# Dilated attention on one core: class keys only where the local scores lack them, counted in the local mask

## Chip, core and metric

The kernel runs on one core of a Trainium2 chip. The metric is the device time of one execution in microseconds (us), as the median of several runs. A profile is one further execution, recorded by the hardware profiler; its own time and its span are given beside the median.

## The reference

One decoder layer on x of 1024 positions by 1024 features, in float32. RMSNorm, one input projection, then two mixers side by side: a gated DeltaNet (4 heads of 128) and a dilated sliding-window attention (8 heads of 64). Their outputs go through one output projection; a gated MLP with a short causal convolution follows, and a last RMSNorm.

The change touches the attention alone. Every query t attends in three branches (window, dilation) = (128, 1), (512, 4), (2048, 16): to the keys t, t−d, t−2d, … back to t−window. The branches are merged by their softmax denominators:

```python
for window, dil in DIL_PATTERNS:
    ...
    num, den, m = band_attention(stride(qf), stride(kf), stride(vf), window // dil)
...
num_tot = wts[0][..., None] * nums[0] + wts[1][..., None] * nums[1] + wts[2][..., None] * nums[2]
den_tot = wts[0] * dens[0] + wts[1] * dens[1] + wts[2] * dens[2]
out = num_tot / den_tot[..., None]
```

With the weights written out this is one softmax over the union of the branches' keys in which a key that m branches want counts m times, that is, in which log m is added to its score. As 1024 positions are shorter than the window of 2048, the third branch reaches back to position 0.

## The kernel before, in words

**Stages.** The input projection comes first, and its products with the DeltaNet's chains; then attention runs beside the rest of the input projection (columns of later head pairs, then the four z columns of the DeltaNet's gate); then the output projection (`out_proj`, L1073), the MLP's up-projection (`mlp_up`, L1306) and down-projection (`mlp_down`, L1556). Big products are done in three passes with operands split in a high and a low part (`mm3`, L196; `split`, L202): names with hi and lo. Products of attention are plain float32 (`mm`, L188), which the profile shows as two records each; a transpose (`tp`, L192) is one record.

**Attention** (`attention`, L879) treats the 8 heads as four pairs (`pi`), and a pair's 1024 queries as 8 blocks of 128 (`n`), in two halves of four (`hh`). Inside a block the positions are ordered by class, that is by t mod 4 (4 classes of 32). Two blocks go through the stages together (`pair`): blocks 0 and 1, 2 and 3, 4 and 5, 6 and 7.

- *Local scores* (`scores`, L898): 128 queries against the keys of their own block and the one before (`n1` columns: 128 for block 0, 256 otherwise), for each of the two heads (`e`), which sit in the two halves of the array's rows.
- *Class scores* (L912): each class's 32 queries against the keys of the same class, in class blocks of 128 keys (class block 0: positions 0 to 511, class block 1: 512 to 1023). `nb` class blocks are taken, 1 in the first half and 2 in the second. There are 4 classes times 2 heads of these products, each on its own 64 by 32 piece of the array.
- *Softmax* (`softmax`, L922; `normalise`, L930): one VectorE operation per head adds the mask to the scores in PSUM and finds the row's extreme, one ACT operation takes the exponential and its sum, VectorE divides (tiles sm and mx). The row is `wd` = `n1` + 128 `nb` long. The local part's mask stands for branch 1, the class part's for branches 2 and 3; there a key wanted by both has 8 log 2 (the scale is 1/8).
- *Turn* (`turn`, L952): the probabilities are transposed in pieces of 128 columns (`wd` / 128 for each head); VectorE copies the local ones to pt, ACT the class ones to pb (`turned`, L944).
- *Values* (`values`, L966): pt times the local values, summed in one PSUM bank (`po`) per half. *Class values* (`merge_classes`, L975): when the half's four blocks are there, pb of all four blocks (128 columns: 4 times 32 queries of one class) against the class's values, for each class, class block and head; the two heads sit in the two halves of the array's columns. `give` (L987) copies the result out (oT).

`advance` (L1002) makes a pipeline: the turn of the pair of blocks before, the scores of this one, the values of the one before.

**What sets the order.** The order of TensorE's instructions is fixed when the program is built. A planner (`Weave`, L46) runs generators as streams with levels; each product adds its cost in us to a clock (`product`, L88), each operation of VectorE, ACT and SP to its engine's (`account`, L78). A stream that yields comes back when its operands should be ready, and the ready stream of the lowest level goes next. Attention has level 5, the input projection (`dense`, L486) level 9, so projection products (ps<-xhi, xlo with whi, wlo in the profile) fill the time in which attention would wait. `mm` stamps each product into that order (L189). The other engines' order is made by the framework's scheduler; attention's operations on VectorE and ACT have high priority there (`uv`, `ua`, L151).

**The end of attention.** `mixer_splits` (L1048) and `out_proj` start in the plan when the input projection is done: `mixer_splits` splits the mixers' outputs (tiles ohi and olo, in the slots of xhi and xlo), `out_proj` loads and splits the output projection's weights (wst<-in_wo, then whi on ACT and wlo on VectorE; two staging slots, two slots each for whi and wlo, and a third pair in slots of pb). The first two output columns are begun with the input parts that are there; the last one is the attention's.

Of the kernel before, what the change touches and what calls it, by code (L numbers as in the profile page):

```python
# [9 lines left out]
AF = mybir.ActivationFunctionType  # L10
# [11 lines left out]
NEG = -1.0e30  # L22
# [122 lines left out]
def hybrid_layer(tc, I, out):  # L145
# [6 lines left out]
    ua = Engine(wv, nc.scalar, "scalar", 0.12, 0.00085, first=tc.high_priority)  # L152
# [35 lines left out]
    def mm(dst, lhs, rhs, us, start=True, stop=True, **kw):  # L188
        tc.stamp_issue_order_token(nc.tensor.matmul(dst, lhs, rhs, start=start, stop=stop, **kw).ins, TOKEN)  # L189
        wv.product(us, dst, lhs, rhs)  # L190
# [54 lines left out]
    def bank(tag, name="ps"):  # L245
        return tile_(pp_, (P, 512), F32, name, tag, 2)
# [602 lines left out]
    def by_block(t):  # L849
        return t.rearrange("p (n c u) -> p n c u", n=NCH, c=4)  # L850
# [25 lines left out]

    HALVES = (slice(0, 64), slice(64, 128))

    def attention():  # L879
        for h in range(2):  # L880
            yield from wv.until(("c", h, NCH - 1))
# [8 lines left out]

        def mask(n):

            i, o, step, w, m = {0: (0, 128, 352, 128, 2), 1: (1, 0, 128, 128, 3), 2: (1, 384, 128, 128, 3),
                                3: (0, 608, 128, 128, 3)}.get(n, (0, 0, 480 - 32 * n, 256, 2))
            t = mks[i]
            return bass.AP(tensor=t.tensor, offset=t.offset + o, ap=[t.ap[0], [step, m], [1, w]]), m

        def scores(pair):  # L898

            for it, tag in zip(pair, ("asc", "atr")):  # L900
                it["k0"] = max(it["n"] - 1, 0) * P
                it["n1"] = (it["n"] + 1) * P - it["k0"]
                it["wd"] = it["n1"] + P * it["nb"]
                it["ps"] = [bank(tag) for _ in range(2)]
            yield wv.need(*pair[0]["ps"], *pair[1]["ps"], pair[0]["q"], pair[0]["k"])
            for it in pair:
                n, k0, n1_ = it["n"], it["k0"], it["n1"]
                for e, er in enumerate(HALVES):
                    mm(it["ps"][e][:, :n1_], it["q"][er, n * P:(n + 1) * P], it["k"][er, k0:k0 + n1_], 0.00085 * n1_)
            for it in pair:  # L910
                n, n1_, wd = it["n"], it["n1"], it["wd"]
                for c in range(4):  # L912
                    o = slice(32 * c, 32 * c + 32)
                    for e, er in enumerate(HALVES):
                        mm(it["ps"][e][o, n1_:wd].rearrange("p (n u) -> p n u", u=32),
                           it["q"][er, n * P + 32 * c:n * P + 32 * c + 32], by_block(it["k"])[er, :4 * it["nb"], c, :],
                           0.00022 * (wd - n1_), tile_position=(64 * e, 32 * c))
                ends = softmax(it)
            while put_off:
                gate(*put_off.pop(0), ends)  # L920
# [23 lines left out]
        def turned(it, e, pt, pp):  # L944
            wd, n1_ = it["wd"], it["n1"]
            inst = uv.tensor_copy(pt[:, :n1_], pp[:, :n1_])
            if it["g"]["pi"] == 3 and it["n"] > 5:
                for lo in last.get("wlo", ()):
                    after(lo, inst, "the probabilities go first")
            ua.activation(it["pb"][e][:, it["u"]].rearrange("p b t -> p (b t)"), pp[:, n1_:wd], AF.Copy)  # L950

        def turn(pair):  # L952
            pts = A("pt", "dv*", shape=(P, 4, 256))
# [21 lines left out]
        def merge_classes(g):  # L975
            vcv = g["vc"].rearrange("p (c b d) -> p c b d", c=4, b=2)
            po, nb = g["po"], g["nb"]
            yield wv.need(*g["pb"], slack=-PSLACK)
            for c in range(4):
                for b in range(nb):  # L980
                    for e in range(2):
                        er = slice(64 * e, 64 * e + 64)
                        mm(po[er].rearrange("p (u t) -> p u t", u=4)[:, :, 32 * c:32 * c + 32],
                           vcv[:, c, b, er], g["pb"][e][:, :, b, 32 * c:32 * c + 32], 0.14,
                           False, c == 3 and b == nb - 1, skip_group_check=True)

        def give(g):  # L987
# [14 lines left out]
        def advance(pair, more=None):  # L1002
            done = pipe.pop() if pipe else None
            if done is not None:
                yield from turn(done)
            if more is not None:
                last["values"] = yield from more
            if pair is not None:
                yield from scores(pair)
                pipe.append(pair)  # L1010
            if done is not None:
                yield from values(done)
                if done[1]["u"] == 3:
                    yield from merge_classes(done[0]["g"])
                    give(done[0]["g"])

        for pi in range(4):
            q, k, vn, vc = cur
            for hh in range(2):
                nb = 1 + hh  # L1020
                if hh == 1 and pi < 3:
                    yield from wv.until(("a", pi + 1, 2))
                    qkv = att_load(pi + 1)
                po = bank("ch")
                pb = [A("pb", "qa", shape=(P, 4, nb, P)) for _ in range(2)]
                if pi == 3 and hh == 1:
                    wv.done.add("last group")
                g = dict(po=po, pb=pb, nb=nb, hh=hh, pi=pi, vc=vc)
                for u in (0, 2):
                    more = att_values(qkv[2]) if (hh, u) == (1, 2) and pi < 3 else None  # L1030
                    yield from advance([dict(n=4 * hh + i, u=i, q=q, k=k, vn=vn, nb=nb, po=po, pb=pb, g=g)
                                        for i in (u, u + 1)], more)
            if pi < 3:
                cur = qkv[:2] + last["values"]
# [583 lines left out]
def host_inputs(inputs):  # L1618
    f = {k: np.asarray(v) for k, v in inputs.items()}
    w = f["w_in"][0]  # L1620
    base = {"q": 0, "k": 512, "v": 1024, "z": 1536}
    cols = [(2056, 2568, 3080)[c[2]] + 128 * c[1] if c[0] == "a" else base[c[0]] + 128 * c[1] for c in DENSE]

    def tile_of(c):
        return w[:, c:c + 128].reshape(8, 128, 128).transpose(1, 0, 2).reshape(128, 1024)
    wi = np.stack([tile_of(c) for c in cols])
    w0 = np.concatenate([w[:, c:c + 128] for c in (512, 640, 768)], axis=1)
    w0 = w0.reshape(4, 2, 128, 384).transpose(0, 2, 1, 3)
    wba = w[:, 2048:2056].reshape(8, 128, 8).transpose(1, 0, 2)
    c4, u32 = np.divmod(np.arange(128), 32)  # L1630
    tq = 4 * u32 + c4
    tk = np.concatenate([tq, tq + 128])
    d = tq[:, None] + 128 - tk[None, :]
    p1 = np.where((d >= 0) & (d <= 128), 0.0, NEG)
    d = u32[:, None] + 224 - np.arange(352)[None, :]
    mult = ((d >= 0) & (d <= 128)).astype(int) + ((d >= 0) & (d % 4 == 0)).astype(int)
    win = np.choose(mult, [NEG, 0.0, 8.0 * np.log(2.0)])
    pad = np.zeros((128, 256))
    mk = [np.concatenate([p1, win, p1, win[:, 128:256], pad[:, :32]], axis=1),
          np.concatenate([p1, win[:, 192:320], p1, win[:, 160:288], pad], axis=1)]  # L1640
    j = np.arange(128)
    a = {
        "xT": f["x"][0].T,
        "n1": f["norm1_w"][0].reshape(8, 128).T,
        "w0": w0, "wi": wi, "wba": wba,
        "gcw": f["conv_qkv_w"][0].reshape(4, 12, 128).transpose(2, 1, 0),
        "a_log": f["a_log"], "dt_bias": f["dt_bias"],
        "gnw": f["gdn_norm_w"][0].reshape(128, 1),
        "wo": f["w_out"][0].reshape(8, 128, 8, 128).transpose(2, 1, 0, 3),
        "n2": f["norm2_w"][0].reshape(8, 128).T,  # L1650
        "wu": f["w_up"][0].reshape(8, 128, 2, 22, 128).transpose(3, 2, 1, 0, 4).reshape(22, 2, 128, 1024),
        "fcw": f["ffn_conv_w"][0].reshape(3, 44, 128).transpose(2, 1, 0),
        "wd": f["w_down"][0],
        "fw": f["final_norm_w"].reshape(8, 128).T,
        "ident": np.eye(128, dtype=np.float32),
        "sel": np.array([[p % 32 == j for j in range(8)] for p in range(128)], np.float32),
        "tri": (j[:, None] <= j[None, :]).astype(np.float32),
        "mk": np.stack(mk).astype(np.float32),
    }
    return {k: np.ascontiguousarray(v) for k, v in a.items()}  # L1660
# [15 lines left out]
```

## Time and profile before

| what | value |
|---|---|
| median of 3 runs | 1232.29 us (1231.43 to 1234.54) |
| the profiled execution, its own time | 1235.56 us |
| its span | 1233.3 us |
| TensorE's mean granted clock over the span | 0.997 |
| DMA, mean over the span | 124 GB/s |

The span runs from the first to the last instruction of the profiled execution. In the profile PE is TensorE's matmuls, PEld its weight loads (they overlap matmuls), DVE VectorE, ACT ScalarE, POOL GpSimd, and SP the engine that issues the DMAs here. A row of the time line has the start, the length, the engine, the line, the operation and the tiles, then how many instructions are merged in it, and in square brackets the idle time before it and what ended that. A group's row has the count, then busy us and the mean ns of one instruction (shared between overlapping ones in the first number), then idle time. Nearly all records have the line of a helper (L189 for products, L193 for transposes, L139 and L141 for the rest), so the tiles tell what they are: ps<-kT,qT are attention's scores, ps<-ident,sm its transposes, ps<-pt,vn the local values, ps<-pb,vc the class values. A matmul's record is longer than the distance to the next one, because they are pipelined; the pace is read from start to start.

### The profile page before, as it was taken

The numbers are of one execution on the slowest core, as the hardware profiler recorded it, in microseconds if no ns is written. First come the engines' busy times: TensorE is split into PE (matmuls) and PEld (weight loads), VectorE is DVE, ScalarE is ACT, GpSimd is POOL, SyncE is SP. The second block draws the span as 40 slices with busy tenths as digits, with TensorE's granted clock in tenths as the row PEclk, the third lists the DMA queues.
The fourth block names the chain that finished last, engine by engine and source line by source line (L and its number), as shares of the span: only waits on it lengthen the run. The fifth ranks groups of instructions, "written<-read, shape, count | busy, mean of one in ns | idle before, by whom it ended". The sixth has DMA issues, their size and how long they took to land.

```text
span 1233.3 us, 18302 instructions
## 1 busy us (share of the span) xinstructions
PE 1215.4 (99%) x7048; PEld 1005.1 (81%) x7048; DVE 967.1 (78%) x1529; ACT 585.5 (47%) x1127; POOL 51.2 (4%) x34
## 2 busy tenths in 40 slices
PE   9999999999999999999999999999999999999996
PEld 7888887898777777888788888888888888888886
DVE  7686984473666777677789888898898979898986
ACT  7383344363444445455454454454444554445451
POOL 0212110022000000000000000000000000000001
PEclk9999999999999999999999999999999999999999
DMA  7423235337442222443331322312213296357733
GB/s 231 103 75 98 86 115 160 103 103 235 133 132 75 104 61 61 140 162 109 112 103 52 103 85 69 103 57 98 101 54 103 77 358 237 106 183 224 238 95 137
DMA packets 81702, 153.52 MB, mean 124 GB/s; under 512 B 21552, under 2 KB 32464, under 8 KB 81616
## 3 DMA queue, kind: packets, MB, share of 16 engines
q1 hardware_dynamic: 81616, 152.37, 37.9%
q8 instruction: 55, 0.90, 0.3%
q14 instruction: 31, 0.25, 0.1%
HBM read 114.31 MB, written 35.93 MB: 122 GB/s over the span
## 4 chain that ended last, share of the span: by engine, by line
PE 94%; DVE 3%; issue 1%; ACT 1%; DMA 0%; POOL 0%; POOLq 0%; DVEq 0%; ACTq 0%
PE ps L189 46%; PE pa L189 19%; PE dw L189 15%; PE pc L189 9%; PE ps L193 4%; DVE x1h L139 1%; DVE pr L139 1%; PE warm L189 1%; DMA wst<-in_wu 0%; DVE rstdB L139 0%; POOL rs L139 0%; DVE olo L139 0%; DVE pt L141 0%; DVE T L139 0%; DVE wst L139 0%
## 5 line engine op out<-in xcount | busy, mean ns | idle before, releaser
L189 PE MATMUL dw<-pr 128*128 128x512 f32 (+1 forms) x984 | 211.3, 376 | 0.0
L189 PEld LDWEIGHTS dw<-pr 128*128 128x128 f32 x984 | 176.6, 188 | 33.6
L189 PE MATMUL ps<-xhi,whi 128*128 128x512 f32 x448 | 187.0, 417 | 0.0
L189 PE MATMUL ps<-xhi,wlo 128*128 128x512 f32 x448 | 176.1, 393 | 0.0
L189 PE MATMUL ps<-xlo,whi 128*128 128x512 f32 x448 | 175.4, 391 | 0.0
L189 PE MATMUL pa<-T,pair 128*128 128x512 f32 x528 | 127.1, 390 | 2.2 <-ACT u L139 2.2
L189 PEld LDWEIGHTS pa<-T,pair 128*128 128x128 f32 x528 | 98.9, 188 | 23.2 <-ACT u L139 2.7
L189 PEld LDWEIGHTS ps<-xhi,wlo 128*128 128x128 f32 x448 | 84.3, 188 | 18.6
L189 PEld LDWEIGHTS ps<-xhi,whi 128*128 128x128 f32 x448 | 84.5, 189 | 17.1 <-issue 3.3
L189 PEld LDWEIGHTS ps<-xlo,whi 128*128 128x128 f32 x448 | 84.8, 189 | 13.2
L139 ACT ACTIVATE u<-pa 128x512 f32<-128x512 f32 x44 | 26.3, 598 | 108.6 <-PE pa L189 108.6
L139 DVE SCALAR_TENSOR_TENSOR y<-xu,fcw,y 128x1023 f32<-128x1023 f32 (+1 forms) x44 | 56.4, 1281 | 24.4 <-ACT y L139 24.4
L139 ACT ACTIVATE pr<-wd 128x1024 fp32r<-128x1024 f32 x33 | 35.0, 1061 | 76.9 <-DVE wd L139 38.2
L139 ACT ACTIVATE whi<-wst 128x1024 fp32r<-128x1024 f32 (+2 forms) x38 | 38.5, 1014 | 60.0 <-PE ps L189 49.8
L189 PE MATMUL pa<-B,A 128*128 128x512 f32 x264 | 63.5, 389 | 0.0
L189 PE MATMUL pc<-B,pair 128*128 128x512 f32 x264 | 63.4, 389 | 0.0
L189 PE MATMUL pc<-T,S 128*128 128x512 f32 x264 | 63.4, 389 | 0.0
L189 PE MATMUL pa<-T,S 128*128 128x512 f32 x264 | 63.4, 389 | 0.0
L141 ACT ACTIVATE sm<-sm,mx 128x512 f32<-128x512 f32 (+2 forms) x64 | 41.2, 646 | 42.2 <-DVE mx L141 42.2
L139 DVE TENSOR_TENSOR wst<-wst 128x512 f32<-128x512 f32 x88 | 60.3, 686 | 0.7
L189 PE MATMUL ps<-B,pair 128*128 128x512 f32 x252 | 60.5, 389 | 0.0
L189 PEld LDWEIGHTS pa<-T,S 128*128 128x128 f32 x264 | 49.5, 188 | 10.3
(233 smaller groups left out, 2312.5 us busy)
## 6 DMA issues: line engine op xcount, KB each, us to landing
wst<-in_wu SPq DMA_DIRECT2D x44, 512.0 KB, 3.7
wd<-in_wd SPq DMA_DIRECT2D x44, 512.0 KB, 4.4
wst<-in_wi SPq DMA_DIRECT2D x25, 512.0 KB, 3.7
upark<-y SPq DMA_DIRECT2D x22, 512.0 KB, 3.7
r<-upark SPq DMA_DIRECT2D x22, 512.0 KB, 9.3
apark<-aqkv SPq DMA_DIRECT2D x12, 512.0 KB, 2.8
wa<-in_wd SPq DMA_DIRECT2D x22, 256.0 KB, 3.0
wst<-in_wo SPq DMA_DIRECT2D x8, 512.0 KB, 4.1
```

The costliest lines, as they stand in the source:

```text
L139: return getattr(eng, op)(*a, **kw)
L141: return getattr(eng, op)(*a, **kw)
L189: tc.stamp_issue_order_token(nc.tensor.matmul(dst, lhs, rhs, start=start, stop=stop, **kw).ins, TOKEN)
L193: tc.stamp_issue_order_token(nc.tensor.transpose(dst, src, ident).ins, TOKEN)
```

## The change

A query block takes class blocks only where the local scores do not hold all of its class keys. `nb` of a block becomes `CBLOCKS[n]` = 0, 0, 1, 1, 1, 1, 2, 2 instead of 1, 1, 1, 1, 2, 2, 2, 2:

- Blocks 0 and 1: their own block and the one before are all keys there are. No class scores; rows of 128 and 256 columns instead of 256 and 384.
- Blocks 4 and 5: class block 1 would hold only keys of blocks 4 and 5, which the local scores have (block 4: the keys of block 4; block 5: those of blocks 4 and 5). Rows of 384 instead of 512.
- The other blocks keep their shape.

The masks follow: the local mask adds 8 log m for a key that m of the three branches want, and the class mask leaves out the keys that the local scores hold. The mask tiles keep their size of 1024 columns each; the positions in them are new.

The probabilities of class blocks that are not taken are not copied to pb, and the class values of a half's last class block run over the last two blocks' queries alone (`us`, 64 columns instead of 128). The planner is given 0.08 us instead of 0.14 for such a product.

```diff
+    CBLOCKS = (0, 0, 1, 1, 1, 1, 2, 2)
...
         def mask(n):
-            i, o, step, w, m = {0: (0, 128, 352, 128, 2), 1: (1, 0, 128, 128, 3), 2: (1, 384, 128, 128, 3),
-                                3: (0, 608, 128, 128, 3)}.get(n, (0, 0, 480 - 32 * n, 256, 2))
+            i, o, step, w, m = ((0, 128, 128, 128, 1), (0, 0, 256, 256, 1), (0, 0, 128, 128, 3), (0, 384, 128, 128, 3),
+                                (1, 0, 128, 128, 3), (1, 384, 192, 128, 3), (1, 0, 736, 256, 2), (1, 0, 704, 256, 2))[n]
...
                 n, n1_, wd = it["n"], it["n1"], it["wd"]
-                for c in range(4):
+                for c in range(4 if it["nb"] else 0):
...
-            ua.activation(it["pb"][e][:, it["u"]].rearrange("p b t -> p (b t)"), pp[:, n1_:wd], AF.Copy)
+            if it["nb"]:
+                ua.activation(it["pb"][e][:, it["u"], :it["nb"]].rearrange("p b t -> p (b t)"), pp[:, n1_:wd], AF.Copy)
...
             for c in range(4):
                 for b in range(nb):
+                    us = slice(2 if b == nb - 1 else 0, 4)
                     for e in range(2):
                         er = slice(64 * e, 64 * e + 64)
-                        mm(po[er].rearrange("p (u t) -> p u t", u=4)[:, :, 32 * c:32 * c + 32],
-                           vcv[:, c, b, er], g["pb"][e][:, :, b, 32 * c:32 * c + 32], 0.14,
+                        mm(po[er].rearrange("p (u t) -> p u t", u=4)[:, us, 32 * c:32 * c + 32],
+                           vcv[:, c, b, er], g["pb"][e][:, us, b, 32 * c:32 * c + 32], 0.14 if us.start == 0 else 0.08,
                            False, c == 3 and b == nb - 1, skip_group_check=True)
...
-                    yield from advance([dict(n=4 * hh + i, u=i, q=q, k=k, vn=vn, nb=nb, po=po, pb=pb, g=g)
+                    yield from advance([dict(n=4 * hh + i, u=i, q=q, k=k, vn=vn, nb=CBLOCKS[4 * hh + i], po=po, pb=pb, g=g)
...
-    p1 = np.where((d >= 0) & (d <= 128), 0.0, NEG)
-    d = u32[:, None] + 224 - np.arange(352)[None, :]
-    mult = ((d >= 0) & (d <= 128)).astype(int) + ((d >= 0) & (d % 4 == 0)).astype(int)
-    win = np.choose(mult, [NEG, 0.0, 8.0 * np.log(2.0)])
+    def logs(mult):
+        return np.where(mult > 0, 8.0 * np.log(np.maximum(mult, 1)), NEG)
+    local = logs(((d >= 0) & (d <= 128)).astype(int) + ((d >= 0) & (d % 4 == 0)) + ((d >= 0) & (d % 16 == 0)))
+    d = u32[:, None] + 224 - np.arange(192)[None, :]
+    far = logs((d <= 128).astype(int) + (d % 4 == 0))
+    strip = np.concatenate([far, np.full((128, 96), NEG)], axis=1)
```

More of the change, by code (lines that the diff above doesn't have):

```diff
@@ L1633, in host_inputs @@
     d = tq[:, None] + 128 - tk[None, :]
-    p1 = np.where((d >= 0) & (d <= 128), 0.0, NEG)
-    d = u32[:, None] + 224 - np.arange(352)[None, :]
-    mult = ((d >= 0) & (d <= 128)).astype(int) + ((d >= 0) & (d % 4 == 0)).astype(int)
-    win = np.choose(mult, [NEG, 0.0, 8.0 * np.log(2.0)])
+    def logs(mult):
[4 more added lines that the diff above has]
+    strip = np.concatenate([far, np.full((128, 96), NEG)], axis=1)
     pad = np.zeros((128, 256))
-    mk = [np.concatenate([p1, win, p1, win[:, 128:256], pad[:, :32]], axis=1),
-          np.concatenate([p1, win[:, 192:320], p1, win[:, 160:288], pad], axis=1)]
     j = np.arange(128)
+    mk = [np.concatenate([local, strip[:, 160:288], local, strip[:, 128:256], pad], axis=1),
+          np.concatenate([local, strip[:, 96:224], local[:, :128], pad[:, :64], local[:, 128:], strip, pad[:, :32]],
+                         axis=1)]
     a = {
```

## The prediction

> **What bounds the kernel now.** I read the page first (span, busy shares, shares of the chain that ended last), then the busy time of each engine in the stretch where attention runs, then what TensorE waited for there.
>
> ```profile
> span 1233.3 us, 18302 instructions
> PE 1215.4 (99%) x7048; PEld 1005.1 (81%) x7048; DVE 967.1 (78%) x1529; ACT 585.5 (47%) x1127; POOL 51.2 (4%) x34
> PE 94%; DVE 3%; issue 1%; ACT 1%; DMA 0%; POOL 0%; POOLq 0%; DVEq 0%; ACTq 0%
> ```
>
> TensorE is busy for 99% of the span, and 94% of the chain is its work. That is an average; the stage decides.
>
> ```profile
> 300.00:400.00 100.00, 100.00 (x879) 79.08 (x878) 62.19 (x161) 41.75 (x108) 0.00 (x0) 1.00 0.39 124
> 400.00:490.00 90.00, 90.00 (x865) 70.83 (x865) 64.42 (x165) 41.73 (x106) 0.00 (x0) 1.00 0.23 72
> 490.00:500.00 10.00, 7.76 (x66) 5.83 (x65) 9.57 (x13) 4.77 (x8) 0.00 (x0) 1.00 0.61 153
> ```
>
> The columns are stretch, length, then busy time of PE, PEld, DVE, ACT and POOL, the granted clock (1.00), DMA share and GB/s. Attention lies here (class scores from 313.16, class values until 495.6, by rows below). Up to 490 TensorE has no idle time at all, since products of the input projection fill the attention's latencies, while VectorE is busy for 62 and 64%. So in this stage a microsecond of TensorE work removed is a microsecond of the run, as long as the fill lasts. Only the end has holes:
>
> ```profile
> PE ps L189 <- DVE pt L141: 1.9, 2, 1.0
> PE ps L189 <- DVE oT L139: 0.4, 1, 0.4
> ```
>
> These are all the waits of TensorE between 300 and 500 us: 2.3 us, by the rows of the tail below all after 490.
>
> **The change, part by part.** There are four groups (head pairs) of eight query blocks, so each saving comes four times.
>
> *Class scores of blocks 0 and 1 go* (16 products per group, two passes each). Rows of the weight loader around the first step:
>
> ```profile
> 313.16 0.40 PEld L189 LDWEIGHTS ps<-kT,qT 64*32 64x32 f32 x32 [0.33 <-issue]
> 313.75 0.19 PEld L189 LDWEIGHTS ps<-xhi,whi 128*128 128x128 f32 x1 [0.20 <-issue]
> ```
>
> Class loads begin at 313.16, after a drain (0.33) that any change of tile shape has; projection products follow at 313.75. Without the class part they would follow the local scores at about 313.16: 0.59 us, times 4 = **2.4 us** (at least the 0.40 of the loads themselves, 1.6).
>
> *Class scores of blocks 4 and 5 are half as wide.* Their step gets the shape that the step of blocks 2 and 3 has now:
>
> ```profile
> 321.28 1.73 PE L189 MATMUL ps<-kT,qT 64*128 64x256 f32 x40
> 322.94 0.88 PE L189 MATMUL ps<-pt,vn 128*64 128x128 f32 x12
> 330.79 2.16 PE L189 MATMUL ps<-kT,qT 64*128 64x256 f32 x40
> 332.87 1.09 PE L189 MATMUL ps<-pt,vn 128*64 128x128 f32 x16
> ```
>
> Start to start, 322.94 − 321.28 = 1.66 with 128 columns and 332.87 − 330.79 = 2.08 with 256: 0.42 us, times 4 = **1.7 us**.
>
> *Eight transposes of probabilities fewer per group* (two each in blocks 0, 1, 4 and 5):
>
> ```profile
> 317.32 0.60 PE L193 MATMUL ps<-ident,sm 128*128 128x128 f32 x4
> 317.67 0.48 PE L189 MATMUL ps<-xhi,whi 128*128 128x512 f32 x1
> 319.15 0.82 PE L193 MATMUL ps<-ident,sm 128*128 128x128 f32 x6
> 337.64 1.03 PE L193 MATMUL ps<-ident,sm 128*128 128x128 f32 x8
> 338.43 0.48 PE L189 MATMUL ps<-xhi,whi 128*128 128x512 f32 x1
> ```
>
> Four take 0.35 and eight 0.79: 0.11 each. (The six projection products between 317.67 and 319.15 take 1.48, 0.25 each with the change of kind; that is used below.) 32 × 0.11 = **3.5 us**. This and the two before are differences of rows of the same kind, so I hold them firm.
>
> *Class values on half the queries.* 8 of 8 products (first half of the blocks) and 8 of 16 (second) now move 64 columns instead of 128. The trace has no such product, so I bound it.
>
> ```profile
> 333.80 1.04 PE L189 MATMUL ps<-pb,vc 128*64 128x128 f32 x16
> 213.57 1.14 PE L189 MATMUL ps<-x,um 64*64 64x64 f32 x16
> L189 PE MATMUL ps<-pb,vc x192: 272/273/273, 333.8 to 495.6; 128*64 128x128 f32 x192
> L189 PE MATMUL ps<-x,um x16: 218/218/267, 213.6 to 214.5; 64*64 64x64 f32 x16
> L189 PEld LDWEIGHTS ps<-pb,vc 128*64 128x64 f32 x192 | 11.0, 137 | 0.0
> ```
>
> The 16 records are 8 products of two passes, and the two heads run side by side in the two column halves: 8 pairs. From first to last start (the length less one record) that is (1.04 − 0.273)/7 = 0.110 us a pair. The nearest row with 64 weight and 64 moving columns is x by um, one at a time: (1.14 − 0.218)/15 = 0.061. Per group 16 pairs become half as wide, 64 in all. Ends: no gain, if the weight loads set the pace (the last row shows the loader without idle time ahead of them), and 64 × 0.055 = 3.5 if the pace halves. A loss is excluded: same weights, fewer columns. I take the x-by-um pace, 64 × (0.110 − 0.061) = **3.1 us**, as that row has the same load and the same columns.
>
> [...]
>
> *Off TensorE*: masking, exponentials, scaling and copies work on 128 elements a row less in four of eight blocks. I cost that at nothing, as TensorE is busy beside all of it; if the fill ended earlier it would be a gain. The masks are one load of the same size.
>
> *The tail.* The planner hands out less projection work per group, so 18 projection products, which ran before the end of attention, now run after it (18 × 0.25 = 4.5 us), and only 3 instead of 6 stand between the last transposes and the last values. The built order shows two more moves. SP issues the last 16 class-value transfers ahead of the first output weight (its slot opens late, so nothing waits). And on ACT and VectorE the split of the third output weight moves from ahead of the last softmax into it.
>
> ```profile
> 479.99 1.06 ACT L139 ACTIVATE whi<-wst 128x1024 fp32r<-128x1024 f32 x1 [1.88 <-DMA wst<-in_wo]
> 481.08 1.22 DVE L139 TENSOR_TENSOR wlo<-wst,whi 128x1024 fp32r<-128x1024 f32 x1 [3.39 <-ACT whi L139]
> 485.09 0.71 ACT L141 ACTIVATE sm<-sm,mx 128x512 f32<-128x512 f32 x1
> 486.12 0.88 DVE L141 TENSOR_SCALAR sm<-sm,mx 128x512 f32<-128x512 f32 x2
> 486.92 1.22 DVE L139 SCALAR_TENSOR_TENSOR zz<-zz,xr 128x1024 f32<-128x1024 f32 x1
> 490.33 0.68 DVE L139 TENSOR_TENSOR xr<-ps,rstdB 128x512 f32<-128x512 f32 x1
> 492.39 1.08 DVE L141 COPY pt<-ps 128x256 f32<-128x256 f32 x3
> wst<-in_wo SPq DMA_DIRECT2D x8, 512.0 KB, 4.1
> ```
>
> ```profile
> 478.55 2.16 PE L189 MATMUL ps<-kT,qT 64*128 64x256 f32 x40
> 488.15 1.03 PE L193 MATMUL ps<-ident,sm 128*128 128x128 f32 x8
> 492.86 1.20 PE L189 MATMUL ps<-pt,vn 128*64 128x128 f32 x13 [1.03 <-DVE pt L141]
> 498.58 0.50 PE L189 MATMUL ps<-ohi,whi 128*128 128x512 f32 x1 [0.39 <-DVE oT L139]
> ```
>
> Count from the last scores (478.55). The first output weight can be split only when the last but one column leaves its slot, three products (0.7) earlier; some 0.3 for the end of the last product (a record of 0.48 outlasts its turn of 0.25), whi 1.06 and wlo 1.22 end near +1.9; only then does the third weight's staging slot open, 4.1 to land (+6.0), whi (+7.1), two exponentials of 0.71 (+8.5), scaling (+9.5). The last transposes stand at 488.15, +9.6: just in time, by 0.1. Then VectorE goes zz, copy, og (as long as zz), copy, xr, two copies: about +13.8, against 493.47 (+14.9) now. The last values may start 1.1 us sooner, of which 0.7 are the three products that come later: 0.4 gained. The 0.39 for oT goes under the 18 products. New is a wait for the second output weight, whose slot opens with the last of those products: 0.3 + 1.06 + 1.22 against eight products of 0.25 ahead of its first use of wlo, 0.6 lost. Sum near **0**, bounds −1.5 and +2.
>
> *Sum*: 2.4 + 1.7 + 3.5 + 3.1 + 0 = 10.7 us. The profiled execution took 1235.56 us (span 1233.3); 10.7 off gives 1224.9. The median of the runs is 1232.29, so I say **1221.6 us**.
>
> **The rivals.**
> 1. *The pace of class values is set by the weight loads.* [...] Against: the x-by-um row. Price 3.1: 10.7 − 3.1 = 7.6, 1224.7 us.
> 2. *The third output weight comes late.* ACT works its queue in order, so the last exponentials stand behind the split that waits for the transfer (above: 0.1 us of slack). Against: TensorE is there only at +9.6. Price if it lands as late as the slowest load of that size:
>
> ```profile
> r<-upark SPq DMA_DIRECT2D x22, 512.0 KB, 9.3
> ```
>
> 9.3 − 4.1 − 0.1 = 5.1 more: 1226.7 us.
>
> 3. *Slower: the softmax chain takes the place of TensorE's work.* Each step's transposes wait for VectorE and ACT, and less TensorE work now lies between scores and transposes. Place: the step of blocks 0 and 1, with no projection product between.
>
> ```profile
> 404.05 0.42 DVE L141 CUSTOM_DVE_ANT_1 sm<-ps,mk 128x256 f32<-128x256 f32 x1 [2.25 <-PE ps L189]
> 405.90 0.62 DVE L141 TENSOR_SCALAR sm<-sm,mx 128x256 f32<-128x256 f32 x2
> 406.88 0.66 PE L193 MATMUL ps<-ident,sm 128*128 128x128 f32 x4
> ```
>
> Probabilities are ready at 406.52, TensorE asks at 406.88: 0.36 of slack, and its cover shrinks by half the class values (8 × 0.049 = 0.4). Against: the chain starts 0.6 sooner, without the class scores, and is shorter. There are 16 steps; slower needs 10.7/16 = 0.67 us of new wait in each. At 1.0 each it is +5.3, 1237.6 us.
>
> 4. *Nothing is gained*: the shorter stage only waits at the next (out-projection operands, its weights), time as before, 1232. Against: the one wait that TensorE has there now is the 0.39 above.
>
> That the change doesn't do what it says is not among them: the built program has 64 class-score products and 32 transposes less, and the narrow class values.
>
> **How the numbers follow.** Forecast, 1218.5 to 1223.5 us (tail from −1.5 to +2, a run's scatter of 1): 0.73. Rival 1: 0.12. Rival 2: 0.06. Rival 3: 0.04. Rival 4: 0.05. The range goes from 1218.0 to 1226.5: it holds the forecast and rival 1, including 2 us of a worse tail, and leaves out about 0.15. A measurement of this kernel tells about 0.3% (3.7 us) from no change: faster by more is forecast, rivals 1 and 2, 0.91; within it rival 4, 0.05; slower rival 3, 0.04.
>
> **What would show it.** Right: the time from the first transposes of probabilities (317.32) to the last scores (478.55), 161.2 now, falls by 9.7 (the sum less the first step's class scores, 0.6, and the last class values, 0.4) and by 3.0 more for twelve projection products that then run elsewhere, to about 148.5; the steps of blocks 0 and 1 have no class loads; four steps of a group have two transposes less; TensorE has no idle time before the last step. [...] Wrong: waits of PE for sm in the steps (rival 3), ACT waiting for wst<-in_wo with PE idle before the last transposes (rival 2), or waits of PE for ohi, olo or wlo well beyond 1 us after attention (rival 4).

## The result, and the profile after

The changed kernel takes **1221.08 us** (median of 4 runs, 1220.84 to 1223.14) against 1233.28 for the kernel before (4 runs beside it, 1231.43 to 1234.54): ratio 0.9895, 95% interval 0.9881 to 0.991, 12.2 us less. Forecast were 1221.6 us and 10.7 us less. All comparisons here are of undisturbed runs. The profiled execution of the changed kernel took 1223.14 us.

The page of the changed kernel, span, busy shares and the chain by engine:

```profile
span 1221.0 us, 17970 instructions
PE 1205.3 (99%) x6888; PEld 997.3 (82%) x6888; DVE 961.7 (79%) x1529; ACT 576.5 (47%) x1111; POOL 50.7 (4%) x34
PE 93%; DVE 3%; issue 1%; DMA 1%; ACT 1%; POOL 0%; POOLq 0%; DVEq 0%; ACTq 0%
```

TensorE is busy for 10.1 us less (1215.4 before), and its share of the span is still 99%: what was taken off it came off the span. 160 of its products are gone: 128 passes of class scores and 32 transposes.

The busy time of the engines by stretch in the attention stage of the changed kernel (columns as above), and TensorE's listed waits between 300 and 500 us:

```profile
300.00:400.00 100.00, 100.00 (x865) 79.21 (x866) 63.43 (x182) 39.42 (x110) 0.00 (x0) 1.00 0.39 123
400.00:470.00 70.00, 70.00 (x671) 55.13 (x670) 51.43 (x138) 31.00 (x84) 0.00 (x0) 1.00 0.25 80
470.00:483.00 13.00, 11.63 (x87) 8.75 (x85) 10.74 (x16) 6.54 (x11) 0.00 (x0) 1.00 0.30 93
```

```profile
PE ps L189 <- DVE pt L141: 1.3, 2, 1.0
```

Until 470 there is still no hole in TensorE. All listed waits of the stretch lie in its last 13 us, as before in the last 10, and they are 1.3 us instead of 2.3.

The first two steps of the changed kernel in the time line:

```profile
309.68 0.52 PEld L189 LDWEIGHTS ps<-kT,qT 64*128 64x128 f32 x8 [0.35 <-issue]
310.54 0.19 PEld L189 LDWEIGHTS ps<-xhi,whi 128*128 128x128 f32 x1 [0.33 <-issue]
...
313.40 0.39 PE L193 MATMUL ps<-ident,sm 128*128 128x128 f32 x2
315.01 0.60 PE L193 MATMUL ps<-ident,sm 128*128 128x128 f32 x4
...
326.44 1.73 PE L189 MATMUL ps<-kT,qT 64*128 64x256 f32 x40
328.11 1.09 PE L189 MATMUL ps<-pt,vn 128*64 128x128 f32 x16
328.92 0.60 PEld L189 LDWEIGHTS ps<-pb,vc 128*64 128x64 f32 x16
329.03 0.63 PE L189 MATMUL ps<-pb,vc 128*64 128x64 f32 x16
```

The step of blocks 0 and 1 has no class loads (64*32) any more: projection products follow at 310.54, 0.86 us after the local scores began. Its transposes are 2 and 4 where 4 and 6 were. The scores of blocks 4 and 5 at 326.44 are now 40 records with 128 class columns, as those of blocks 2 and 3 were, and take 328.11 − 326.44 = 1.67 us. The class values move 64 columns: sixteen records in 0.63.

To compare the stage as a whole I take the time from the first local scores to the first product of the output projection, 312.30 to 495.85 = 183.55 us before and 309.68 to 482.28 = 172.60 after, called **the stage** below. Both kernels run the same number of projection products (417) in it. By kind of product, from one start to the next, summed over the trace's records (a wait is counted with the product before it, so most of the +0.85 of the local values is a wait of 0.8 us that the kernel before has behind projection products):

| kind | before, us | after, us | difference |
|---|---|---|---|
| scores, local and class | 29.68 | 25.07 | −4.61 |
| transposes of probabilities | 21.11 | 17.65 | −3.46 |
| class values | 11.48 | 8.17 | −3.31 |
| local values | 16.20 | 17.05 | +0.85 |
| projection | 102.69 | 102.29 | −0.40 |
| values' own transposes | 2.39 | 2.38 | −0.01 |
| stage | 183.55 | 172.60 | −10.95 |

One step is like the next: in each of the four groups the scores of blocks 0 and 1 went from 1.45 to 0.86 us, those of blocks 4 and 5 from 2.09 to 1.66, the class values of the first half from 0.97 to 0.56, and of the second from 1.85 to 1.44 (except where the tail begins). The spans differ by 12.3 us, 1.35 more than the stage. That is 2.6 us which the profile of before lost near 207 us against that of after (1.4 of them a longer wait, the rest a dip of the clock), and 1.3 that the profile of after lost near 583. Both lie outside the stage, on products that the two kernels share (last section).

### The profile page after: what moved, and what is told of

The parts are those of the page before. It is cut to its first block, busy times and chain, and to the rows that moved or that the text cites. A ratio compares the mean times of both kernels' runs of the same rounds, so it can differ in the third digit from the quotient of the medians.

```text
span 1221.0 us, 17970 instructions
## 1 busy us (share of the span) xinstructions
PE 1205.3 (99%) x6888; PEld 997.3 (82%) x6888; DVE 961.7 (79%) x1529; ACT 576.5 (47%) x1111; POOL 50.7 (4%) x34
## 4 chain that ended last, share of the span: by engine, by line
PE 93%; DVE 3%; issue 1%; DMA 1%; ACT 1%; POOL 0%; POOLq 0%; DVEq 0%; ACTq 0%
PE ps L189 45%; PE pa L189 19%; PE dw L189 15%; PE pc L189 10%; PE ps L193 3%; DVE x1h L139 1%; DVE pr L139 1%; PE warm L189 1%; DMA wst<-in_wu 0%; DVE rstdB L139 0%; POOL rs L139 0%; DMA wst<-in_wo 0%; DVE sm L141 0%; DVE pt L141 0%; DVE zz L139 0%
## 5 line engine op out<-in xcount | busy, mean ns | idle before, releaser
L141 ACT ACTIVATE sm<-sm,mx 128x384 f32<-128x384 f32 (+3 forms) x64 | 37.8, 592 | 45.5 <-DVE mx L141 45.5
```

What stands on the lines that cost most here:

```text
L141: return getattr(eng, op)(*a, **kw)
```

## The experiments

The theory: **TensorE's stream of instructions is the bound, and each removed piece is worth its own time on TensorE.** Against it stand the rivals of the prediction (pace of the loads, a late weight in the tail, the softmax chain) and a planner whose new order might have made part of the gain. Each kernel was run beside the kernel before; ratios are to that. The medians of the kernel before went from 1233.3 to 1235.1 us over these measurements, so terms of a microsecond or two are read from the stage in the profile, and not from the run.

**1. The class values alone** (the kernel before, with `us`).

```diff
                 for b in range(nb):
+                    us = slice(2 if b == nb - 1 else 0, 4)
```

> The kernel before, with the narrow class values alone (all class scores and transposes stay; the class values of the first two blocks are left out in the last class block of each half, so part of the attention's result is missing). Measure: the time from the first local scores to the first out-projection product, 183.55 us in the profile of before. Theory (columns set the pace, 0.058 us for a narrow pair against 0.110): 64 pairs x 0.051 = 3.3 us less, 180.3, and the run 3.3 less, ratio 0.9973. Rival 1 (weight loads set the pace): 183.5, ratio 1.000. A third reading, that the narrow class values gained through the planner's new order and not through their own time: the steps of class values would take their 0.97 and 1.85 us as before, and the gain would be in waits.

1230.61 us, ratio 0.9963 (0.9949 to 0.9976); the stage 180.77 us, 2.8 less than before. The class values of a first and of a second half in its time line:

```profile
330.60 0.63 PE L189 MATMUL ps<-pb,vc 128*64 128x64 f32 x16
...
357.31 1.51 PE L189 MATMUL ps<-pb,vc 128*64 128x128 f32 x32
```

Sixteen narrow passes take 0.63 instead of the 1.04 of the kernel before; in the second row narrow and wide ones alternate (it has the shape of its first). From start to start the steps took 0.56 and 1.44 us as in the changed kernel, so 4 × 0.82 = 3.3 us are theirs. The stage gave 0.5 less, by waits that the list of TensorE's waits does not hold: the scores at 400.34 took 1.78 us instead of 1.45, and at 456.41 the weight loader waited 0.48 us for ACT's copy to pb, where the kernel before had 0.32 (at 457.71). Rival 1 as priced (no gain) is refuted, and so is a gain through the order alone.

**2. Blocks 0 to 3 alone** (blocks 4 and 5 stay at two class blocks, with masks to fit).

```diff
-    CBLOCKS = (0, 0, 1, 1, 1, 1, 2, 2)
+    CBLOCKS = (0, 0, 1, 1, 2, 2, 2, 2)
...
-                    us = slice(2 if b == nb - 1 else 0, 4)
+                    us = slice(2 if nb == 1 else 0, 4)
```

> The change for blocks 0 to 3 alone: no class scores and no class transposes of blocks 0 and 1, narrow class values in the first half; blocks 4 and 5 keep 256 class columns and the second half its wide class values. Theory (each piece is worth its own TensorE time): 4 x (0.59 class scores + 0.44 transposes + 0.41 class values) = 5.8 us less than before, the interval 177.8 of 183.55, ratio 0.9953. Rival (what gained is the shorter softmax chain, and it is needed in every step): the part of blocks 0 and 1 would bring what its steps no longer wait, and they waited for nothing before: near 0, ratio 1.000.

1227.9 us, ratio 0.9936 (0.9911 to 0.9961); the stage 176.60, 7.0 less. The steps: scores of blocks 0 and 1 0.86 us, of blocks 4 and 5 2.09 as before, the transposes of blocks 0 and 1 2 and 4 instead of 4 and 6, class values 0.56 and 1.85. That is the 5.8 expected. The other 1.1 are waits: 0.5 of them is one that the kernel before had at 457 us, and the rest came from the tail, which had 0.6 us of listed waits instead of 2.3.

**3. The removed TensorE work given back to the changed kernel**, into columns that nobody reads.

```diff
-                for c in range(4 if it["nb"] else 0):
+                wx = n1_ + P * it["g"]["nb"]
+                for c in range(4):
...
-                        mm(it["ps"][e][o, n1_:wd].rearrange("p (n u) -> p n u", u=32),
+                        mm(it["ps"][e][o, n1_:wx].rearrange("p (n u) -> p n u", u=32),
...
+                    for i in range(wd // P, n1_ // P + it["g"]["nb"]):
+                        tp(pp[:, i * P:(i + 1) * P], sm[:, e, :P])
```

> The changed kernel, with the removed class scores (blocks 0 and 1, second class block of 4 and 5) and the removed transposes computed again into columns that nobody reads; masks, exponentials, scaling, copies and narrow class values stay as changed. Theory (TensorE's stream is the bound): 4 x (0.59 + 0.43 + 0.87) = 7.6 us come back, the interval 180.2 instead of 172.6, the run near 1228.7 (ratio to before 0.9972). Rival (the shorter work of VectorE and ACT made part of the gain): the interval stays well under 180, at 172.6 if it made all of it.

1227.9 us, ratio 0.994 (0.9921 to 0.9959); the stage 178.50. Scores 29.17 (+4.1 on the changed kernel) and transposes 21.05 (+3.4) came back to what they were before, apart from the wait of 0.5 at 457 us: 7.5 of the 7.6 expected. The stage rose by 5.9 only, since the tail's waits went from 1.3 listed (plus the lateness that experiments 9 and 10 show) to 0.6. The short softmax is still in place here, so it made none of these 7.5. That it brought nothing of its own is not shown, though: this kernel has the same products as that of experiment 1, and its stage is still 2.3 us shorter (178.50 against 180.77). Whether the shorter softmax did that or the order which the planner made with it, no run separates.

**4. The planner's cost.**

```diff
-                           vcv[:, c, b, er], g["pb"][e][:, us, b, 32 * c:32 * c + 32], 0.14 if us.start == 0 else 0.08,
+                           vcv[:, c, b, er], g["pb"][e][:, us, b, 32 * c:32 * c + 32], 0.14,
```

> The changed kernel, with the planner's cost of a narrow class value at 0.14 as for a wide one (a number that only moves projection products between the steps). Theory (moved products cost the same where they land): the interval moves only by the products that leave or enter it, 0.245 us each, and the run stays within 1 us of the changed kernel's 1221.1. Rival (the planner's new order is part of the gain): 2 us or more slower.

1221.53 us (1220.84 to 1222.34), ratio 0.9887 (0.9868 to 0.9906): no difference that the runs can tell. The moved products cost the same elsewhere. The stage is 1.4 shorter (171.20), again by the tail's waits (0.6 us).

**5, 6, 11. How near is the softmax chain?** (rival 3). More passes of VectorE over the exponentials in every block, which the planner does not see; TensorE's order stays that of the changed kernel.

```diff
+            with tc.high_priority(offset=URGENT):
+                for e in (1,):
+                    nc.vector.tensor_scalar(sm[:, e, :wd], sm[:, e, :wd], 1.0, None, op0=OP.mult)
             uv.reciprocal(den, den)
```

With `(0, 1)` for two passes and `(0, 1, 0, 1)` for four.

> The changed kernel, with one more pass of VectorE over the second head's exponentials (times 1.0) in every block, unseen by the planner: the softmax chain is longer by 0.24 us (128 columns) to 0.44 (512) in each of 32 blocks, 11 us of VectorE work in all, more than the change took away. By the trace of the changed kernel the probabilities are ready 0.8 to 3.4 us before TensorE asks for them, except in two steps (0.19 and 0.15). Theory: only these two wait, 0.2 + 0.3 = 0.5 us more, run within 1 us of 1221.1. Rival 3 (the chain sets the pace): 16 steps x 0.35 = 5.6 us more.

> The same with four passes (two for each head): the chain is longer by about 0.96, 1.24, 1.5 and 1.76 us for 128, 256, 384 and 512 columns. Theory (a step waits by what exceeds its own slack in the trace of the changed kernel): 0.3 in blocks 0, 2.3 in blocks 2 and 3, 1.2 in blocks 5, 1.6 in the last block: about 5 us more than the changed kernel, between 3 and 8 as VectorE also gets busier. Rival 3 (every step pays the full length): 16 x 1.5 = 24 us more. If the fill can absorb all of it: under 1 us.

One pass: 1222.84 us, ratio 0.9902 (0.9884 to 0.9921), the stage 172.76, +0.2. Four: 1243.68 us, ratio 1.0067 (1.0047 to 1.0087), the stage 193.55, **+21**. TensorE's waits between 300 and 500 us, with one pass and then with four:

```profile
PE ps L189 <- DVE pt L141: 1.2, 1, 1.2
PE ps L193 <- DVE sm L141: 0.5, 2, 0.4
```

```profile
PE ps L193 <- DVE sm L141: 13.3, 22, 2.7
PE ps L189 <- ACT pb L141: 1.2, 2, 0.6
PE ps L189 <- DVE xr L139: 1.1, 1, 1.1
```

One pass is what I expected, two short waits for sm. Four are not: 22 waits for sm, and 21 us where 5 were expected and 24 were the rival's. My slack model fell. It took each block by itself, though both blocks of a step stand in one VectorE queue. A new theory, and a run for it:

> The changed kernel with two extra passes of VectorE in every block (one for each head), between the kernel with one pass (time from the first scores to the first out-projection product 172.76 us, 0.2 more than the changed kernel) and the one with four (193.55, 21 more, where 5 was expected). New theory: the two blocks of a step share VectorE, so the second one is late by its own passes and by what the first one's passes push it back, less the pause of about 0.3 us between them; with d = 0.62 and 0.75 us (256, 384 columns) the second block is late by 0.8 to 1.25, which is over the slack only in three steps (slack 0.19, 0.79 and 0.15 by the trace of the changed kernel): 1.1 + 0.5 + 0.7, about 2 us more, 1 to 4. If instead each added pass costs in each step alike (21 us for four), two cost about 10 us. If only more than a fixed reserve costs and it is over one pass, between 5 and 8.

1225.86 us, ratio 0.993 (0.9909 to 0.9951); the stage 176.12, +3.5: within what was expected (1 to 4), above the 2 in its centre. Its waits for sm, and then a step in which work of the projection stands ahead of the second block (L944 are the added passes):

```profile
PE ps L193 <- DVE sm L141: 3.1, 5, 1.4
```

```profile
405.60 1.12 DVE L139 TENSOR_TENSOR aqkv<-ps,rstdB 128x512 f32<-128x512 f32 x1
...
407.47 1.21 DVE L139 TENSOR_TENSOR wlo<-wst,whi 128x1024 fp32r<-128x1024 f32 x1
...
408.61 0.15 DVE L141 RECIPROCAL mx<-mx 128x2 f32<-128x2 f32 x1
408.68 0.33 DVE L944 TENSOR_SCALAR sm<-sm 128x384 f32<-128x384 f32 x1
...
409.82 1.18 PE L193 MATMUL ps<-ident,sm 128*128 128x128 f32 x6 [0.80 <-DVE sm L141]
```

The same place in the changed kernel:

```profile
405.23 1.22 DVE L139 TENSOR_TENSOR wlo<-wst,whi 128x1024 fp32r<-128x1024 f32 x1
...
406.37 0.15 DVE L141 RECIPROCAL mx<-mx 128x2 f32<-128x2 f32 x1
406.56 0.75 DVE L141 TENSOR_SCALAR sm<-sm,mx 128x384 f32<-128x384 f32 x2
407.17 0.82 PE L193 MATMUL ps<-ident,sm 128*128 128x128 f32 x6
```

The second block's last operations stand behind work of the projection (aqkv, wlo of 1.2 us) in VectorE's order. In the changed kernel that leaves 0.2 us, with two passes it is 0.8 late. So the reserve of the chain is real but small and uneven. By its records an added pass takes 0.33 us on 384 columns (above): one in each block costs 0.2 us in all, two cost 3.5, four cost 21. That both blocks share the queue is shown; how much of the 21 us each effect made is not separated.

**7. What sets the pace of a narrow pair?** One block of two.

```diff
-                    us = slice(2 if b == nb - 1 else 0, 4)
+                    us = slice(3 if b == nb - 1 else 0, 4)
```

> The changed kernel, with the narrow class values of one block instead of two (32 moving columns instead of 64 in 64 pair-passes; blocks 2 and 6 lose the last class block's share, so part of the attention's result is missing). It asks what sets the pace of the narrow pairs, 0.058 us with 64 columns. If the weight loads do (64 columns each, 0.055 us apart where loads stand alone): no gain, the pair stays near 0.055, the interval at 172.4 or more. If the moving columns do: 0.03 a pair, 64 x 0.028 = 1.8 us less, 170.8.

1221.56 us, ratio 0.9904 (0.9875 to 0.9933); the stage 172.27, 0.3 less than the changed kernel's. Loads and products of the first narrow class values in this kernel:

```profile
328.67 0.60 PEld L189 LDWEIGHTS ps<-pb,vc 128*64 128x64 f32 x16
328.78 0.61 PE L189 MATMUL ps<-pb,vc 128*64 128x32 f32 x16
```

Half the columns, and the loads take the same 0.60, the products 0.61 instead of 0.63. So the moving columns do not set the pace of the narrow pairs; the weight loads, which stayed as they were, fit. A fixed cost of each product would look the same here and is not told apart. Narrowing ended where the prediction's 64 columns are: the step from 64 to 32 is worth 0.2 us in all.

**8, 9, 10. The tail** (rival 2). The changed kernel again, beside one whose last exponentials go ahead of the third output weight's split on ACT, and one whose last copies of probabilities also go ahead of zz and og on VectorE.

```diff
+                last["thi"] = ac.activation(third[0], st, AF.Copy)
...
+            if it["g"]["pi"] == 3 and it["n"] == 7:
+                last["exp"] = exp
+                if "thi" in last:
+                    after(last["thi"], exp, "the exponentials go first")
```

In the third kernel also:

```diff
+        last["zz"] = insts[1]
...
+            if it["g"]["pi"] == 3 and it["n"] == 6:
+                after(last["zz"], inst, "the probabilities go first")
+            if it["g"]["pi"] == 3 and it["n"] == 7:
+                if "tlo" in last:
+                    after(last["tlo"], inst, "the probabilities go first")
```

> The changed kernel again, beside the two that follow: 1221, ratio to before 0.9895. It also shows whether the stretch of half granted clock (3.4 us, once in each profile) stays at its place: if it belongs to the program it falls on the same instructions again.

> The changed kernel, with the last block's exponentials ahead of the split of the third output weight on ACT, which waited 2.07 us for its transfer with them behind it. Theory (in the changed kernel this wait cost only what the last transposes were late, 0.15 to 0.4 us, and the waits for pt that follow come from zz and og ahead of the copies on VectorE): 0 to 0.4 us gained. Rival 2 (ACT's late split is what holds the tail): all of the tail's 1.3 to 1.7 us of waits go.

> As the kernel with the exponentials first, and VectorE copies the last turned probabilities ahead of zz, og and the third weight's second half. Theory: TensorE's waits for pt before the last values (1.3 us, and 0.4 at the last transposes) go, the run is 1.0 to 1.7 us under the changed kernel. Rival: the wait only moves on to the out-projection's operands (ohi, olo behind og), and nothing is gained.

| kernel | median, us | ratio to before (95%) | stage, us |
|---|---|---|---|
| changed, again | 1222.84 | 0.9913 (0.9898 to 0.9928) | 172.76 |
| exponentials first | 1220.26 | 0.9886 (0.9874 to 0.9899) | 170.61 |
| copies first too | 1220.89 | 0.9892 (0.9877 to 0.9906) | 170.63 |

The tail of the changed kernel (its first profile) on ACT, VectorE and TensorE:

```profile
468.11 1.06 ACT L139 ACTIVATE whi<-wst 128x1024 fp32r<-128x1024 f32 x1 [2.07 <-DMA wst<-in_wo]
469.07 0.71 ACT L141 ACTIVATE sm<-sm,mx 128x512 f32<-128x512 f32 x1
469.20 1.22 DVE L139 TENSOR_TENSOR wlo<-wst,whi 128x1024 fp32r<-128x1024 f32 x1 [1.95 <-ACT whi L139]
...
470.81 0.88 DVE L141 TENSOR_SCALAR sm<-sm,mx 128x512 f32<-128x512 f32 x2
471.44 1.06 PE L193 MATMUL ps<-ident,sm 128*128 128x128 f32 x8
471.61 1.22 DVE L139 SCALAR_TENSOR_TENSOR zz<-zz,xr 128x1024 f32<-128x1024 f32 x1
472.75 0.42 DVE L141 COPY pt<-ps 128x256 f32<-128x256 f32 x1
...
474.68 0.65 PE L189 MATMUL ps<-pt,vn 128*64 128x128 f32 x6 [1.03 <-DVE pt L141]
475.61 0.87 PE L189 MATMUL ps<-pt,vn 128*64 128x128 f32 x7 [0.28 <-DVE pt L141]
```

And with the exponentials first:

```profile
467.44 0.71 ACT L141 ACTIVATE sm<-sm,mx 128x512 f32<-128x512 f32 x1
468.48 0.89 DVE L141 TENSOR_SCALAR sm<-sm,mx 128x512 f32<-128x512 f32 x2
469.10 1.04 ACT L139 ACTIVATE whi<-wst 128x1024 fp32r<-128x1024 f32 x1
...
472.04 1.03 PE L193 MATMUL ps<-ident,sm 128*128 128x128 f32 x8
472.68 0.75 DVE L141 COPY pt<-ps 128x256 f32<-128x256 f32 x2
473.70 1.60 PE L189 MATMUL ps<-pt,vn 128*64 128x128 f32 x15
```

In the changed kernel ACT stands for 2.07 us before the split, with the last exponentials queued behind it: VectorE has their scores and extremes ready at 466.25, and they start at 469.07, with the split before them on ACT. The probabilities of the last block are ready at 471.69 and VectorE, late by that, gets to the copies last: TensorE waits 1.03 and 0.28 us for pt. With the exponentials first the probabilities are ready at 469.37, and TensorE has no listed wait left in the stage; the stage is 2.0 us shorter than in the first profile of the changed kernel and 2.2 shorter than in the second. Expected of my theory were 0 to 0.4, and of rival 2 the 1.3 to 1.7 of all waits, so **my reading of the tail fell and rival 2's held**; the gain is even above its 1.7. Putting the copies ahead of zz and og as well added nothing: with the exponentials first no listed wait was left for it to take. The run is 2.6 us under the changed kernel beside it, but 0.8 under the first measurement of the changed kernel; the ratios' intervals touch or overlap (0.9874 to 0.9899 against 0.9898 to 0.9928 and 0.9881 to 0.991). The stage's 2 us are shown, in both kernels; that the run is shorter by as much is likely, not shown.

## Why the prediction was right

*The bound.* TensorE's stream in a stage without holes: right. Experiment 3 gives the work back without the softmax, and the scores and transposes are back to within 0.1 us, the wait of 0.5 at 457 us apart.

*Class scores of blocks 0 and 1*, 2.4 us forecast: 4 × 0.59 = 2.4. *Of blocks 4 and 5*, 1.7: 4 × 0.43 = 1.7. (The table's 4.61 has 0.5 more. In one step of blocks 2 and 3, at 457.09, the scores of the kernel before took 2.18 us instead of 1.66: the weight loader waited there for ACT's copy to pb, which the list of TensorE's waits does not hold.) *Transposes*, 3.5: 3.46. These were differences of rows of the same kind in the same trace, and nothing had to be assumed. The weight loader's pause after the local scores, which the forecast of the class scores left in place, stayed: 0.33 us at all 16 places of both profiles, whether class scores, values or projection products follow. At other changes of tile shape it has other lengths (0.17 us between the class values and the projection products of before). Common to 102 of the 103 changes before and 98 of the 99 after is that the first load of the new shape starts 0.07 us before the record of the last product ends; loads of one shape start 0.2 us or more before that (medians by shape).

*Class values*, 3.1: 3.3. The pace is (0.63 − 0.222)/7 = 0.058 us a pair (16 records of 0.222 in 0.63) where the x-by-um row gave 0.061. The row with the same load and the same columns was the right one to borrow. **Rival 1** was wrong in its price; its cause may well be right: halving the columns again left the pace where it was (experiment 7), but at 0.058 us a pair, and not at the 0.110 that the pairs with 128 columns took. The loads of the two heads start 7 ns apart, and those of the next pair 58 ns after them, while products of the pair before run (last section).

*Off TensorE*, costed at nothing: right where TensorE has no hole. For the waits in the steps and in the tail it is open, by the 2.3 us between experiments 1 and 3.

*The tail*, 0 with bounds −1.5 and +2: near in sum, but not by its parts. From the last scores to the first product of the output projection it took 20.65 us instead of 17.30. Fifteen more projection products of 0.235 make +3.5 of that and the narrow class values −0.4, so the tail itself lost 0.2 us, where a gain of 0.4 had been counted. The 18 products did take the place of the wait for oT (its 0.39 is gone), and of the 0.6 for the second output weight some 0.4 came (the products at 483.23 and 484.63 start 0.26 and 0.14 late). The step that failed is the count of the third weight's split, "just in time, by 0.1": whi ended 7.5 us after the last scores instead of 7.1, the scaling 10.1 instead of 9.5, the last transposes began 0.2 us late (the product ahead of them began at 471.00 and takes 0.23; they began at 471.44), and TensorE then waited 1.3 us for the copies behind them. With the exponentials ahead of the split the stage is 2 us shorter (experiment 9). **Rival 2** was therefore real. Its price of 5.1 supposed the slowest load of that size; the case here was a split that began at +6.5 instead of +6.0. It hardly hurt the forecast, which counts only the change: the kernel before had waits of much the same size in its tail (1.9 us for pt).

*Rival 3*: the chain's reserve was read as 0.36 us in a step of blocks 0 and 1. In the changed kernel the divided probabilities of that place are ready 0.9 us before TensorE asks for them, where it was 0.6 (each head by itself), so there the change went the safe way. It is tight elsewhere: in two blocks, at 407.17 and 471.44, only 0.2 us are left. Experiments 5, 6 and 11 show how little more the chain can take.

*Rival 4*: the out-projection had no waits that took the gain back, apart from the 0.4 us for its second weight; its first product came 13.6 us earlier in the profile and what follows kept 12.3.

*The check named in the prediction*: from the first transposes to the last scores 148.5 us were forecast; it is 313.40 to 461.63 = 148.2. The wait of 0.5 us at 457 us, which is gone, is part of that and was not in the count.

*The 10.7 against 12.2 measured*: the stage gave 10.95. The rest is outside the stage and differs from one measurement to the next; the second one of the changed kernel (experiment 8) gave 11.4 us between the medians.

## What to carry to other kernels

Where the bounding engine has no hole in a stage, take durations from rows of the same kind and add them; such terms held to 0.1 us here, while the one place where several engines wait for each other, the tail, needed an experiment. Slack that is read off one trace is not a budget: what stands behind in the same queue shifts too. In 30 of 32 blocks of the changed kernel the probabilities were ready 0.8 us or more before TensorE asked for them, and still two added passes in each block, of 0.33 us each on 384 columns, cost 3.5 us. A transfer that an engine waits for is to be priced by what is queued behind it, even if the engine itself is idle half of the time: ACT is 47% busy here, and putting the last exponentials ahead of its wait of 2.07 us took 2 us off the stage.

## What the runs showed of the hardware

*A pair of weight loads into the two column halves took the time of a single one, 0.058 us.* In the changed kernel's records of the narrow class values the loads of the two heads, each 64 columns into its own half of the columns and on the same 128 rows, start 7 ns apart and take 138 ns each; the next two follow 58 ns later, while products of the pair before are running. The pair's pace is 0.058 us with 64 moving columns and with 32, and 0.110 with 128. Single loads of 64 columns with their products (x by um, in the prediction) follow each other 58 ns apart as well, in the profile of before.

*The granted clock fell to 0.50 for 3.4 us, at 207.5 us in the profile of before and at 583.2 in that of after.* Before and during the dip in the profile of the kernel before, and then in that of the changed one:

```profile
204.10:207.50 3.40, 1.95 (x65) 1.34 (x56) 0.00 (x0) 0.04 (x1) 0.00 (x0) 1.00 0.14 52
207.50:210.90 3.40, 3.40 (x54) 2.36 (x54) 0.68 (x1) 1.24 (x4) 0.00 (x0) 0.50 0.50 157
```

```profile
579.80:583.20 3.40, 2.92 (x22) 2.64 (x20) 3.30 (x7) 2.04 (x4) 0.00 (x0) 1.00 0.01 2
583.20:586.60 3.40, 3.15 (x7) 2.48 (x8) 3.30 (x6) 1.77 (x3) 1.33 (x1) 0.50 0.00 0
```

The last number but two is the granted clock: 0.50 in the second row of each, after a stretch in which TensorE was busy for 1.95 and 2.92 of 3.40 us. A thin stretch did not bring the dip by itself: in the second profile of the same changed kernel (experiment 8) TensorE is busy for only 2.70 us between 583.20 and 586.60, and the clock stays at 1.00 there and in the 3.4 us that follow. It also stays at 1.00 from 203 to 212 there, where the profile of before has its dip. With four added passes (experiment 6) it was 0.51 from 491.90 to 495.30. (The last 9 us of each profile are left out here.) So the dip did not fall on the same instructions again, which was the question of experiment 8. By estimate, from a clock of 0.50 over 3.4 us, a dip takes up to half of that, 1.7.

For a forecast: the spans of two profiles differed by 2 us with no difference in the kernel (1221.0 and 1219.1 for the changed one), so a term below that is read from the stage and not from the span.
